# Half products in banks of their own, and q's low part behind the scans, in a hybrid decoder layer on Trainium2

## The chip, the cores and the metric

The kernel runs on one core of a Trainium2 chip. A core has a matmul engine (PE, with PEld for its weight loads), a vector engine (DVE), a scalar engine (ACT), a general engine (POOL) and a sync engine (SP), which here issues nearly all DMAs. Each engine works through its own instructions in order, and waits on semaphores for the others. SBUF is the memory on the chip; the results of matmuls go to PSUM, which is divided into banks. The metric is the device time of one execution in microseconds (us).

## The reference

One layer over 1024 tokens with 16 meta tokens ahead (1040 positions) and width 1024. After a norm, one projection feeds two groups of heads, 16 heads of an SSD (a state space scan in chunks of 128) and 16 heads of attention. An output projection over both and a convolutional FFN of width 2816 follow. The change lies in the projections q, k, v and in the attention, which has no softmax: each key takes its share of what the keys nearer to the query have left.

```python
xn = rms_norm(h, mix_pre_g[l])
proj = xn @ w_in[l]
q = proj[..., OFF_Q:OFF_K].reshape(Bsz, L, SB_HEADS, SB_HEAD_DIM)
...
    def block(args):
        i, qi = args
        ...
        zlog = jnp.einsum('bqhd,bkhd->bhqk', qi, kp) * scale
        log_beta = jax.nn.log_sigmoid(zlog)
        log_keep = jnp.where(valid, log_beta - zlog, 0.0)
        after = lax.cumsum(log_keep, axis=3, reverse=True) - log_keep
        w = jnp.where(valid, jnp.exp(log_beta + after), 0.0)
        return jnp.einsum('bhqk,bkhd->bqhd', w, vp)
...
mix = jnp.concatenate([y_ssd, y_sb], axis=-1) @ w_out[l]
h = h + rms_norm(mix, mix_post_g[l])
```

## The kernel before, in words

**Precision.** Matmuls take operands in a rounded 32-bit form. Where one product would be too coarse, an operand is split into a high part (a rounded copy, by ACT) and a low part (the rest, by DVE or POOL), and three products are added: high by high, high by low, low by high. So x, the weights, q and k all come as pairs (`wh`/`wl`, `qh`/`ql`, `kh`/`kl`).

**Stages.** Up to about 40 us x is loaded and normed. From 40 to 158 us come the convolved inputs of the SSD and its gate z for the first half of its heads; from 158 to 300 us the first scan of the SSD, with projections of the second half between; from 335 to 458 us its second scan, with the first 35 steps of the q, k, v products between. From 454 to 939 us the attention of the head pairs 0 to 6 runs, with the other q, k, v steps as filling; from 939 to 1018 us that of pair 7, with products of the output projection as filling. The rest of the output projection and the FFN follow to the end at 1855 us; the change does not touch them.

**The q, k, v products.** q, k and v of eight head pairs are 24 products of 1024 x 128 weights with x, taken two at a time as a `Blocks` object, twelve in all. Each goes by a scheme with 7 half-size products in place of 8. Products 1, 2 and 3 use x as it stands in SBUF (resident); 6, 5, 7 and 4 use sums of parts of x, `t2`, `t1`, `t3` and `t4`. These `x_sums` are worked out once, ahead of the first scan, written to DRAM (`xt13`, `xt42`), and streamed back through a ring of two places, each loaded in two halves (`load_half`, line 398); a matmul step asks for the next half when it has used one. Each product has two column halves of 260, so a block has 14 steps of 12 matmuls. The order of products is that of the list `QKV`: 1, 2, 6, 5, 3, 7, 4. Products 2, 5, 3 and 4 need sums of others: some are added in DVE when a PSUM bank is emptied, others by matmuls that go on in a bank that is kept. For k, the high part is copied from the bank by ACT and the low part taken by DVE (line 473) from the bank.

**Weights of a block.** `load` (line 407) brings 512 KB for each of the two, `split_a`, `sums`, `split_s12`, `split_s34` and `split_a22` make the weights of the products from them: the high part by ACT (line 413), the low part by POOL (line 414), sums by DVE (lines 429 to 432). A buffer of raw weights is loaded anew when POOL has taken the last low part from it.

**Attention.** For pair p and block i of 128 queries, `block_weights` multiplies q's block with all keys up to it (z, line 940; three products for each of two heads, in chunks of keys; 7 ends in two groups of chunks). ACT makes two sigmoids of each z (`kp` line 941, `bt` line 942). `split_q` takes the parts of the next block's q (`qh` on ACT, `ql` on DVE, line 917). DVE runs along the keys for the two heads (the scans, line 948), and POOL multiplies (line 950). Two blocks later `block_turn` transposes `bt` (`tw`, line 962), ACT copies it (`th`, line 964), and `block_mix` multiplies it with v (line 977). `edge_turn` and `edge_mix` do the meta keys, and store a pair's result (line 1001).

**Order.** PE's order in the attention is written out by hand, by the order of the code: `manual_schedule` for PE alone. On DVE, ACT, POOL and SP a scheduler orders the instructions.

Of the kernel before, what the change touches and what calls it, by code (L numbers as in the profile page):

```python
# [44 lines left out]
QKV = [(1, "a11", "b11", True), (2, "a12", "b21", False), (6, "s2", "t2", True), (5, "s1", "t1", True),  # L45
       (3, "s4", "b22", False), (7, "s3", "t3", True), (4, "a22", "t4", False)]
# [11 lines left out]
def tile_layer(ctx: ExitStack, tc: tile.TileContext, x, meta, rows, parts,  # L58
# [292 lines left out]
    def behind(*engines):  # L351
        st = ExitStack()
        traced = nc.cur_bb.bb.instructions
        for e in engines:
            last = next((i for i in reversed(traced) if i.engine == e), None)
            if last is not None:
                st.enter_context(tc.issue_after(last))
        return st

    def x_sums(k):  # L360
        rs = []

        def add_up():
            rs.extend(rp.tile([P, 2, HT], F32R, tag="rkl", name=f"xr{j}_{k}", bufs=3).bitcast(F32) for j in range(2))
            r1, r2 = rs
            with behind(ET.Pool):
                for r, kk in ((r1, k), (r2, k + 4)):
                    nc.gpsimd.tensor_tensor(r, xq[:, kk, :, 0].bitcast(F32), xq[:, kk, :, 1].bitcast(F32), op=ALU.add)
                nc.gpsimd.tensor_tensor(r1[:, 0], r1[:, 1], r1[:, 0], op=ALU.subtract)
                nc.gpsimd.tensor_tensor(r1[:, 1], r2[:, 1], r1[:, 1], op=ALU.subtract)  # L370

        def split():
            r1, r2 = rs
            with behind(ET.DVE, ET.Activation):
                nc.vector.tensor_tensor(r2[:, 1], r2[:, 1], r1[:, 0], op=ALU.subtract)
                nc.vector.tensor_tensor(r2[:, 0], r2[:, 0], r2[:, 1], op=ALU.subtract)
                for r, dst, nm in ((r1, xt13, "13"), (r2, xt42, "42")):
                    h = rp.tile([P, 2, HT], F32R, tag="rk", name=f"xh{nm}_{k}", bufs=3)
                    lo = r.bitcast(F32R)
                    nc.scalar.activation(h, r, AF.Copy)  # L380
                    nc.vector.tensor_tensor(lo, r, h.bitcast(F32), op=ALU.subtract)
                    for j, s in enumerate((h, lo)):
                        nc.sync.dma_start(out=dst[:, :, :, k, j, :],
                                          in_=s.bitcast(F32).rearrange("p t (c n) -> p t c n", n=HP))

        return add_up, split

    ring = [xq[:, 0:4, 1].rearrange("p k b n -> p k (b n)")[:, :, 2 * HP * s:2 * HP * s + 2 * HP] for s in range(2)]
# [3 lines left out]
    def load_half():  # L392
        u, h = divmod(loaded[0], 2)
        if u < len(units):
            loaded[0] += 1
            (src, j), c = t_of[units[u][0]], units[u][1]
            ks = slice(2 * h, 2 * h + 2)
            nc.sync.dma_start(out=ring[u % 2][:, ks].bitcast(F32), in_=src[:, j, c, ks].rearrange("p k b n -> p k (b n)"))

    class Blocks:  # L400
        def __init__(self, f1, f2, n):
            self.n, self.src, self.w = n, [{"q": w_q, "k": w_k, "v": w_v}[f][p] for f, p in (f1, f2)], {}
            self.f, self.r, self.late = (f1, f2), [None, None], []
# [21 lines left out]
        def sums(self):  # L425
            r1, r2 = self.r
            self.s2 = rp.tile([P, 4, P], F32, tag="s2", name=f"s2_{self.n}", bufs=1)
# [36 lines left out]
        def part(self, j, th, c):  # L464
            a = HT * th + HP * c
            if self.f[j][0] == "k":
                return [t[:, a:a + HP] for t in self.d[j]]
            return self.d[j][:, a:a + HP]

        def keep_k(self, th, c, a):  # L470
            kh, kl = self.part(0, th, c)
            acts = [lambda: nc.scalar.activation(kh, a, AF.Copy),
                    lambda: nc.vector.tensor_tensor(kl, a, kh.bitcast(F32), op=ALU.subtract)]
            if th == 0:
                acts.pop(0)()
            self.late += acts

        def step(self, s):
            (n, wn, xn, first), c = QKV[s // 2], s % 2
            if s == 0:  # L480
                self.d = [None, self.dest(1)]
            if s == 2:
                self.d[0] = self.dest(0)
            if first:
                self.acc = getattr(self, "acc", {})
                self.acc[c] = psum_mm(f"pj{n}_{self.n}_{c}")
            acc = self.acc[c]
            hi, lo = self.w[wn]
            if xn[0] == "t":
                rv = ring[used[0] % 2].rearrange("p k (b n) -> p k b n", b=2)  # L490
                used[0] += 1
            else:
                kk, th = {"b11": (0, 0), "b21": (4, 0), "b22": (4, 1)}[xn]
                rv = xq[:, kk:kk + 4, th, :, HP * c:HP * c + HP]
            for k in range(4):
                for j, (w, b) in enumerate(((hi, 0), (hi, 1), (lo, 0))):
                    mm(acc[:, :HP], w[:, k, :], rv[:, k, b, :], start=first and k == 0 and j == 0,  # L497
                       stop=k == 3 and j == 2, skip_group_check=not first)
                if xn[0] == "t" and k % 2:
                    load_half()  # L500
            for act in self.late:
                act()
            self.late = []
            add, a = nc.vector.tensor_tensor, acc[:, :HP]
            c11 = self.part(0, 0, c) if n in (2,) else None
# [1554 lines left out]
```

## Time and profile before

| what | value |
|---|---|
| median of 3 runs | 1852.49 us (1851.43 to 1856.2) |
| profiled execution, own time | 1856.6 us |
| its span, first to last instruction | 1854.8 us |
| mean granted clock of PE | 0.968 |
| PE busy | 1729.7 us (93%) |
| DVE, ACT, POOL busy | 1233.3, 856.6, 972.9 us |
| scans L948, 128 instructions | 209.4 us on DVE |
| products L950, 128 instructions | 210.2 us on POOL |
| q, k, v matmuls L497, weights `whis` | 768 instructions, 169.9 us |
| ring loads of x-sums | 192 loads of 520 KB |

A row of a timeline has the start in us from the span's beginning, the length in us, engine, line, operation, the tiles (written <- read), their shapes, and how many stand together; in brackets is how long the engine was idle before it, and what ended that. Rows of groups have busy time and mean duration in ns, and after the next bar the idle time ahead of them. Rows of waits have the sum, the number of times and the longest, in us. In rows of the profile, `kp`, `q` and `xall` are names without their numbers; the ring lies in `xall`, and the streamed sums are `xt`.

### The profile page before, as it was taken

What the parts mean: (1) busy time and instruction counts of PE and PEld (TensorE: products, weight loads), DVE (VectorE), ACT (ScalarE), POOL (GpSimd) and SP (SyncE); (2) the same over time, 40 slices, a digit from 0 to 9 for tenths busy, and PEclk for the clock granted to TensorE, in tenths of its full rate; (3) what the DMA queues carried; (4) which work ended last, traced back from release to release, by engine and by line L of the source; (5) the groups of instructions that cost most, each with busy time, mean ns of one, the idle gap of its engine ahead of it and who ended that gap; (6) DMA issues with size and microseconds to landing.
All of it is one profiled execution on the core that took longest, in us unless ns stands there. A gap on an engine that the chain in (4) does not pass through costs nothing. (4 is left out here: it accounts for less than half of the span.)

```text
span 1854.8 us, 29414 instructions
## 1 busy us (share of the span) xinstructions
PE 1729.7 (93%) x11518; PEld 1508.0 (81%) x11518; DVE 1233.3 (66%) x1360; ACT 856.6 (46%) x1474; POOL 972.9 (52%) x697
## 2 busy tenths in 40 slices
PE   7999899997888889888899999999999999999998
PEld 6998789876777788777767877898888999888786
DVE  5765884776658758768764056766666666657777
ACT  5424463543555656546665234543333333334544
POOL 4365664575657747667546212458677777600001
PEclk9999899998999989999999999999999999999999
DMA  4235443677665556655722354423223333187335
GB/s 153 69 109 177 146 132 103 206 251 244 216 199 185 196 158 200 218 201 192 239 92 83 133 198 148 137 69 117 95 86 92 118 103 104 61 270 251 103 97 187
DMA packets 151354, 284.73 MB, mean 154 GB/s; under 512 B 14032, under 2 KB 47336, under 8 KB 151216
## 3 DMA queue, kind: packets, MB, share of 16 engines
q1 hardware_dynamic: 151216, 282.85, 46.3%
q8 instruction: 91, 1.49, 0.3%
q14 instruction: 47, 0.39, 0.1%
HBM read 224.56 MB, written 58.25 MB: 152 GB/s over the span
## 5 line engine op out<-in xcount | busy, mean ns | idle before, releaser
L950 POOL TENSOR_TENSOR bt<-bt,kp 128x256 f32<-128x256 f32 (+7 forms) x128 | 210.2, 1660 | 139.9 <-DVE kp L948 110.3
L948 DVE TENSOR_TENSOR_SCAN kp<-kp,hold 128x272 f32<-128x272 f32 (+7 forms) x128 | 209.4, 1676 | 64.6 <-ACT kp L941 47.6
L497 PE MATMUL pj<-xall,whis 128*128 128x260 f32 x768 | 169.9, 319 | 53.0 <-DMA xall<-xt 35.1
L497 PEld LDWEIGHTS pj<-xall,whis 128*128 128x128 f32 x768 | 131.3, 209 | 69.3 <-issue 26.0
L1413 POOL TENSOR_TENSOR wlo<-wr,whi 128x1024 fp32r<-128x1024 f32 x43 | 109.2, 2551 | 37.2 <-ACT whi L1412 37.2
L497 PE MATMUL pj<-xall,whia 128*128 128x260 f32 x576 | 116.3, 300 | 10.2 <-DMA xall<-xt 6.2
L1917 POOL TENSOR_TENSOR fms<-fms 128x1 f32<-128x1 f32 x8 | 2.7, 334 | 223.7 <-DMA ar<-fda 187.5
L497 PE MATMUL pj<-xall,wlos 128*128 128x260 f32 x384 | 116.2, 303 | 0.0
L941 ACT ACTIVATE kp<-z 128x288 f32<-128x288 f32 (+6 forms) x112 | 82.5, 737 | 67.5 <-PE z L940 33.0
L497 PEld LDWEIGHTS pj<-xall,whia 128*128 128x128 f32 x576 | 89.8, 192 | 21.0 <-issue 6.0
L1412 ACT ACTIVATE whi<-wr 128x1024 fp32r<-128x1024 f32 x43 | 45.6, 1060 | 112.5 <-PE fX L1470 68.1
L160 PE MATMUL pj_X<-xall,wh_X 128*128 128x320 f32 (+1 forms) x384 | 96.9, 338 | 0.0
L1542 DVE SCALAR_TENSOR_TENSOR ga<-gr,pp,ga 128x1024 f32<-128x1024 f32 x44 | 71.4, 1622 | 34.0 <-ACT ga L1535 33.1
L964 ACT ACTIVATE th<-tw 128x1024 f32<-128x1024 f32 (+2 forms) x96 | 75.8, 815 | 39.2 <-PE tw L962 37.9
L160 PE MATMUL pj_z<-xall,wh_z 128*128 128x306 f32 (+2 forms) x384 | 92.4, 327 | 0.0
L1802 ACT ACTIVATE dh<-ar 128x512 fp32r<-128x512 f32 x77 | 48.5, 630 | 92.5 <-PE dnB L1880 44.7
L1803 DVE TENSOR_TENSOR dl<-ar,dh 128x512 fp32r<-128x512 f32 x77 | 53.2, 691 | 50.4 <-ACT dh L1802 50.3
L1119 PE MATMUL mo<-xall,yh 128*128 128x512 f32 x256 | 85.7, 402 | 0.0
L962 PE MATMUL tw<-ident,bt 128*128 128x128 f32 x576 | 78.7, 280 | 5.4 <-ACT bt L942 3.1
L942 ACT ACTIVATE bt<-z 128x288 f32<-128x288 f32 (+6 forms) x112 | 82.8, 740 | 0.0
L497 PE MATMUL pj<-xall,wloa 128*128 128x260 f32 x288 | 81.7, 284 | 0.0
L497 PEld LDWEIGHTS pj<-xall,wlos 128*128 128x128 f32 x384 | 80.3, 209 | 0.0
(579 smaller groups left out, 5752.6 us busy)
## 6 DMA issues: line engine op xcount, KB each, us to landing
xall<-xt SPq DMA_DIRECT2D x192, 520.0 KB
wr<-in_w_up SPq DMA_DIRECT2D x44, 512.0 KB
fds<-ga SPq DMA_DIRECT2D x44, 256.0 KB
b<-in_w_down SPq DMA_DIRECT2D x44, 256.0 KB
ar<-fds SPq DMA_DIRECT2D x44, 256.0 KB
fda<-ga SPq DMA_DIRECT2D x33, 256.0 KB
ar<-fda SPq DMA_DIRECT2D x33, 256.0 KB
yk<-yd SPq DMA_DIRECT2D x16, 512.0 KB
```

Source lines behind the costliest of these rows:

```text
L160: mm(acc[:ncol, :n - s], a[:, k, :ncol], x_cols(k, b, c0 + s, n - s), start=(k == 0 and j == 0), stop=(k == KB - 1 and j == 2))
L497: mm(acc[:, :HP], w[:, k, :], rv[:, k, b, :], start=first and k == 0 and j == 0, stop=k == 3 and j == 2, skip_group_check=not first)
L941: nc.scalar.activation(kp[:, :, a:a + w], z[:, :, :w], AF.Sigmoid, scale=-QSCALE)
L942: nc.scalar.activation(bt[:, :, a:a + w], z[:, :, :w], AF.Sigmoid, scale=QSCALE)
L948: nc.vector.tensor_tensor_scan(kp[:, j][:, ::-1], kp[:, j][:, ::-1], hold[:, L - n:L][:, ::-1], 0.0, op0=ALU.mult, op1=ALU.max)
L950: nc.gpsimd.tensor_tensor(bt[:, j, 0:m], bt[:, j, 0:m], kp[:, j, 1:m + 1], op=ALU.mult)
L962: nc.tensor.transpose(tw[:, j, b, :], bt[:, j, c0:c0 + P], ident)
L964: nc.scalar.activation(th[:, :, :nb, :], tw[:, :, :nb, :], AF.Copy)
L1119: mm(acc, u[:, k, :], v[:, cs], start=(k == 0 and j == 0), stop=(k == 7 and j == 2))
L1413: nc.gpsimd.tensor_tensor(l, raw, h.bitcast(F32), op=ALU.subtract)
L1542: nc.vector.scalar_tensor_tensor(v, self.g[jj][:, :, i:i + 256], fconv_w[:, j, i:i + 1], v, op0=ALU.mult, op1=ALU.add)
L1803: sub(lo[:, k], raw, hi[:, k].bitcast(F32), op=ALU.subtract)
```

## The change

- The products come in the order 6, 5, 3, 7, 1', 4, 2', two columns halves each, where 1' and 2' are the next block's. The first block's products 1 and 2 run ahead. Each product has a PSUM bank of its own; the sums between products are made by DVE adds when the bank is emptied.
- k's two halves are added into an SBUF tile `ks`; ACT copies its high part, 520 columns at once, and POOL takes the low part.
- `load`, the splits and the sums of the next block's weights stand at other steps. A half of the ring is one stretch of 4160 bytes per partition, where it was two of 2080.
- `x_sums` is wholly on DVE, and the code asks for it in the stage ahead of the scan.
- In the attention the written order counts for PE, DVE, ACT and POOL (`ORDERED`); SP's stays with the scheduler. `split_q` of the next block stands behind the scans. The store of a pair's result is put off to a later place in the loop.

```diff
     def x_sums(k):
-        rs = []
-        def add_up():
...
-        def split():
...
+        tag, dt_, w = (("rkl", F32R, L), ("rq", F32, L + 3))[k % 2]
+        r1, r2 = (rp.tile([P, w], dt_, tag=tag, name=f"xr{j}_{k}", bufs=3)[:, :L].bitcast(F32)
+                  .rearrange("p (t n) -> p t n", t=2) for j in range(2))
+        op2 = nc.vector.tensor_tensor
+        for r, kk in ((r1, k), (r2, k + 4)):
+            op2(r, xq[:, kk, :, 0].bitcast(F32), xq[:, kk, :, 1].bitcast(F32), op=ALU.add)
...
-    ring = [xq[:, 0:4, 1].rearrange("p k b n -> p k (b n)")[:, :, 2 * HP * s:2 * HP * s + 2 * HP] for s in range(2)]
+    ring = [xq[:, a, 1].rearrange("p b n -> p (b n)") for a in range(4)]
...
+        def keep_k(self, th, c, a, term):
+            if c == 0:
+                self.ks = rp.tile([P, HT], F32, tag="s2", name=f"ks{th}_{self.n}", bufs=1)
+            nc.vector.tensor_tensor(self.ks[:, HP * c:HP * c + HP], a, term, op=ALU.add)
+            if c == 1:
+                kh, kl = (t[:, HT * th:HT * th + HT] for t in self.d[0])
+                nc.scalar.activation(kh, self.ks, AF.Copy)
+                nc.gpsimd.tensor_tensor(kl, self.ks, kh.bitcast(F32), op=ALU.subtract)
...
-            if first:
-                self.acc = getattr(self, "acc", {})
-                self.acc[c] = psum_mm(f"pj{n}_{self.n}_{c}")
-            acc = self.acc[c]
+            acc = psum_mm(f"pj{n}_{self.n}_{c}")
...
+            for dst, term in {6: ((c21, c21),), 5: ((c22, c21),), 7: ((c22, c22), (c21, c21)), 4: ((c21, c21),)}[n]:
+                nc.vector.tensor_tensor(dst, a, term, op=ALU.add)
...
         for n, b in enumerate(blocks):
+            row = [(b, 6), (b, 5), (b, 3), (b, 7)] + ([(nxt, 1), (b, 4), (nxt, 2)] if nxt else [(b, 4)])
+            acts = {1: [b.split_a22]}
...
+                acts.update({4: [nxt.split_a], 7: [nxt.sums], 9: [nxt.split_s12], 12: [nxt.split_s34]})
+            if n and nxt:
+                acts[2] = [lambda: nxt.load(0)]
+                acts[5] = [lambda: nxt.load(1)]
...
-        nxt = (p, i + 1) if i < NT - 1 else (p + 1, 0)
-        if nxt[0] in heads:
-            split_q(*nxt)
         m = n - NM
         for j in range(2):
             nc.vector.tensor_tensor_scan(kp[:, j][:, ::-1], kp[:, j][:, ::-1], hold[:, L - n:L][:, ::-1], 0.0,
...
         turn.append((p, i, bt))
+        nxt = (p, i + 1) if i < NT - 1 else (p + 1, 0)
+        if nxt[0] in heads:
+            split_q(*nxt)
...
-        nc.sync.dma_start(out=yd1[:, :, p, :].rearrange("t d c -> d t c"), in_=ysc)
+        stores.append(lambda: nc.sync.dma_start(out=yd1[:, :, p, :].rearrange("t d c -> d t c"), in_=ysc))
...
-    pe_order.enter_context(tc.manual_schedule(engines={mybir.EngineType.PE}))
+    pe_order.enter_context(tc.manual_schedule(engines=ORDERED))
...
             run(block)
+            while stores:
+                stores.pop()()
```

DVE in the attention of pair 5. In the names, the first number is the pair (of `pj`, the product) and the second the block; `kp` rows are the two scans, `ql` is q's low part, `q7` and `vt6` are evacuations of q, k, v products. Before:

```order
L948 SCALAR_TENSOR_TENSOR kp5_4_8583<-kp5_4_8583,hold_4355 128x656 x2
L917 TENSOR_TENSOR ql5_6_8677<-q5_6831,qh5_6_8676 128x128
L948 SCALAR_TENSOR_TENSOR kp5_5_8656<-kp5_5_8656,hold_4355 128x784 x2
L514 TENSOR_TENSOR q7_8543<-pj6_10_0_8693,q7_8543 128x260
L917 TENSOR_TENSOR ql5_7_8761<-q5_6831,qh5_7_8760 128x128
L514 TENSOR_TENSOR q7_8543<-pj6_10_1_8720,q7_8543 128x260
L948 SCALAR_TENSOR_TENSOR kp5_6_8740<-kp5_6_8740,hold_4355 128x912 x2
```

and now:

```order
L937 SCALAR_TENSOR_TENSOR kp5_4_8659<-kp5_4_8659,hold_4374 128x656 x2
L909 TENSOR_TENSOR ql5_5_8685<-q5_6827,qh5_5_8684 128x128
L491 TENSOR_TENSOR vt6_8694<-pj2_10_0_8695,q7_8537 128x260
L491 TENSOR_TENSOR vt6_8694<-pj2_10_1_8722,q7_8537 128x260
L937 SCALAR_TENSOR_TENSOR kp5_5_8736<-kp5_5_8736,hold_4374 128x784 x2
L909 TENSOR_TENSOR ql5_6_8762<-q5_6827,qh5_6_8761 128x128
L494 TENSOR_TENSOR q7_8537<-pj6_10_0_8773,q7_8537 128x260
L494 TENSOR_TENSOR q7_8537<-pj6_10_1_8800,q7_8537 128x260
L937 SCALAR_TENSOR_TENSOR kp5_6_8820<-kp5_6_8820,hold_4374 128x912 x2
L909 TENSOR_TENSOR ql5_7_8846<-q5_6827,qh5_7_8845 128x128
```

Before, the low part of block 6 stood ahead of the scans of block 5; now it stands right behind them.

SP, which issues the loads, around the weights of block 10 (`wr0` and `wr1` are its two raw weights, rows with `xt13` and `xt42` the ring's halves, `yd1` a stored result). Before:

```order
L398 DMA xall_126<-xt13_109 128x2x520 x8
L1001 DMA yd1_92<-ysc3_6974 128x8x128
L398 DMA xall_126<-xt42_110 128x2x520 x8
L407 DMA wr0_10_8122<-in_w_v 128x1024
L558 DMA mvd_111<-v5_8017 16x128
L407 DMA wr1_10_8334<-in_w_q 128x1024
L398 DMA xall_126<-xt13_109 128x2x520 x8
```

and now:

```order
L993 DMA yd1_92<-ysc3_7030 128x8x128
L380 DMA xall_126<-xt42_110 128x1040 x8
L529 DMA mvd_111<-v5_8122 16x128
L389 DMA wr0_10_8342<-in_w_v 128x1024
L380 DMA xall_126<-xt13_109 128x1040 x4
L389 DMA wr1_10_8453<-in_w_q 128x1024
L380 DMA xall_126<-xt13_109 128x1040 x4
```

No load of the ring stood between the two weight loads; now four do.

DVE at the start of the first scan, whose first operations are `xdt`, `xw` and `cbm`; `xr` and `xh` belong to `x_sums`, with k as the second number. Before:

```order
L642 COPY xtk0_3_1215<-tt_X03_2_1225 128x512
L375 TENSOR_TENSOR xr1_0_1320<-xr1_0_1320,xr0_0_1319 128x520
L376 TENSOR_TENSOR xr1_0_1320<-xr1_0_1320 128x520
L794 TENSOR_TENSOR xdt0_0_1591<-xk0_0_1564,dt_652 16x512
L820 TENSOR_TENSOR xw0_0_1715<-xdt0_0_1591,dec_676 16x512
L794 TENSOR_TENSOR xdt0_1_1657<-xk0_1_1630,dt_652 128x512
L381 TENSOR_TENSOR xr0_0_1319<-xr0_0_1319,xh13_0_1413 128x1040
```

and now:

```order
L365 CAST xh13_3_1554<-xr0_3_1546 128x1040
L361 TENSOR_TENSOR xr1_3_1547<-xr1_3_1547 128x520
L366 TENSOR_TENSOR xr0_3_1546<-xr0_3_1546,xh13_3_1554 128x1040
L365 CAST xh42_3_1559<-xr1_3_1547 128x1040
L366 TENSOR_TENSOR xr1_3_1547<-xr1_3_1547,xh42_3_1559 128x1040
L788 TENSOR_TENSOR xdt0_0_1591<-xk0_0_1564,dt_652 16x512
L814 TENSOR_TENSOR xw0_0_1715<-xdt0_0_1591,dec_676 16x512
```

Before, the sums of k = 0 were begun when the scan began; now those of the last k = 3 end ahead of it.

More of the change, by code (lines that the diff above doesn't have):

```diff
@@ L499, in step @@
                 if xn[0] == "t" and k % 2:
                     load_half()
[L501 to L505, printed above, removed]
+            a = acc[:, :HP]
             c21, c22 = self.part(1, 0, c), self.part(1, 1, c)
@@ L572, in qkv_flow, with turn_next @@
         post = []
+        def turn_next():
+            act = post.pop(0) if post else None
+            if act:
+                act()
+        first = blocks[0]
+        for n in (1, 2):
+            for c in range(2):
+                first.step(n, c)
+                if n == 2 and c == 0:
+                    first.split_s34()
+                yield
         for n, b in enumerate(blocks):
@@ L1221, in tile_layer @@
     edge_mix(7, edge)
+    stores.pop()()
     run(meta_steps)
```

167 lines of the change are left out of this document (68 added, 99 removed).

## The prediction, made before the changed kernel ran

> **What bounds the kernel now.** I read the table of windows first, to find the stages in which PE (the matmul engine) has room. Its columns are the window, its length, the busy time of PE, of its weight loads, of DVE, ACT and POOL, the granted clock, and the DMA engines' share and rate.
>
> ```profile
> 100.00:165.00 65.00, 62.02 (x392) 60.92 (x390) 34.19 (x24) 15.98 (x25) 36.55 (x19) 0.97 0.43 142
> 165.00:230.00 65.00, 53.15 (x298) 46.13 (x299) 53.61 (x47) 34.57 (x67) 44.25 (x29) 0.84 0.48 149
> 458.00:936.00 478.00, 411.45 (x3641) 368.86 (x3641) 345.29 (x381) 276.79 (x504) 312.20 (x222) 0.93 0.60 199
> 936.00:1020.00 84.00, 81.68 (x603) 60.92 (x601) 42.95 (x38) 48.59 (x87) 45.37 (x35) 0.98 0.24 77
> ```
>
> From 458 to 936 us (attention of the pairs 0 to 6, with the q, k, v products as fill) PE is idle for 478.00 - 411.45 = 66.6 us. At a mean clock of 0.93 it also loses 0.07 x 411.45 = 28.8 us. So 95 us is the most that this stage could give up while PE's work stays the same. From 165 to 230 us (start of the first scan of the SSD half) the same count gives 11.9 + 8.5 = 20.4 us. Against that, 100 to 165 us shows an undisturbed stretch: 3.0 + 1.9 = 4.9 us. The last window has only 2.3 us idle.
>
> Second, the waits of PE from 458 to 936 us, by what came last (sum, times, longest), and the waits of SP's sequencer, which issues the loads, from 335 to 936 us:
>
> ```profile
> PE pj L497 <- DMA xall<-xt: 39.0, 24, 5.7
> PE pj L497 <- DVE kl L473: 14.4, 9, 2.9
> ...
> SPq L407 <- POOL wlos L414: 61.9, 10, 12.5
> SPq L407 <- POOL wloa L414: 57.6, 7, 16.1
> ```
>
> PE waits mostly for the ring of x-sums (39.0 us), then for k's low part, which frees a PSUM bank (14.4 us). Behind the ring stands SP: it is parked for 61.9 + 57.6 us at weight loads whose buffer POOL's split has yet to leave, and the ring's loads queue behind them. The timeline has such a case, SP first, then PE (start, length, engine and line):
>
> ```profile
> 590.19 0.35 SPq L407 DMA_DIRECT2D wr<-in_w_q  x1
> 590.63 1.92 SPq L398 DMA_DIRECT2D xall<-xt  x4
> 595.35 0.77 PE L497 MATMUL pj<-xall,whis 128*128 128x260 f32 x2 [5.47 <-DMA xall<-xt]
> ```
>
> The weight load goes at 590.19, four ring loads follow at once, and PE starts at 595.35 after 5.47 us of idleness.
>
> **The change part by part.** *Ring, banks, weight loads: -95 us at most.* The streamed products now alternate with resident ones, so a ring half has two more steps to arrive. Each product owns its bank, and DVE adds the parts afterwards, so k's low part holds no bank any more. Between the two weight loads of a block, and before the first, more ring loads go first, as the order of SP shows. I take the whole 95 us out and put back what remains: 9 us of ring and bank waits (at least 4; at most 25, about half of 39.0 + 14.4).
>
> *The cost of own banks.* DVE has 168 evacuations for 152, 16 more. The row of the same size:
>
> ```profile
> L473 DVE TENSOR_TENSOR kl<-pj,kh 128x260 fp32r<-128x260 f32 x26 | 10.9, 418 | 3.1 <-ACT kh L472 3.1
> L368 POOL TENSOR_TENSOR xr<-xall 128x1040 f32<-128x1040 f32 x8 | 21.7, 2722 | 6.5 <-DMA xt<-xr 5.2 <-DVE em L791 1.3
> ```
>
> 16 x 0.418 = 7 us lie beside PE, DVE being busy for 345 of 478 us; I cost them at nothing, 7 us if the cover is gone. k's high part on ACT now comes behind two such adds, and what is queued on ACT behind it waits too, the sigmoids of a z block among them. 16 halves x 0.42 = 6.7 us; I take 6 (2 to 10). POOL gets 16 subtractions of 520 columns, at half of the second row's 2.72 us some 22 us in all. POOL is busy for 312 of 478 us and nobody needs k's low part before the next pair: nothing, and within the 2 to 10 if that fails.
>
> *q's low part behind the scans: +79 us.* Before, q's low part for block i+1 stood on DVE between the scans of i-1 and of i. Now it stands behind the two scans of block i, and since DVE works in written order, PE's z of block i+1 waits for it. That closes a loop: z of i, sigmoids on ACT, two scans, low part of q, z of i+1. I read its length from the timeline of before. PE's z rows (start of z for i = 4, the low-part matmul in it, then i = 5, 6; after the break i = 6, 7 and 0 of the next pair):
>
> ```profile
> 836.91 0.42 PE L940 MATMUL z<-kh,qh 64*128 64x328 f32 x2
> 837.17 0.32 PE L940 MATMUL z<-kh,ql 64*128 64x328 f32 x2
> 842.33 0.45 PE L940 MATMUL z<-kh,qh 64*128 64x392 f32 x2
> 848.35 0.48 PE L940 MATMUL z<-kh,qh 64*128 64x456 f32 x2
> ...
> 779.74 0.47 PE L940 MATMUL z<-kh,qh 64*128 64x456 f32 x2
> 787.23 0.42 PE L940 MATMUL z<-kh,qh 64*128 64x348 f32 x2
> 794.92 0.34 PE L940 MATMUL z<-kh,qh 64*128 64x144 f32 x2
> ```
>
> and DVE's scans (both of a block in one row) and low parts:
>
> ```profile
> 839.77 4.81 DVE L948 TENSOR_TENSOR_SCAN kp<-kp,hold 128x656 f32<-128x656 f32 x2 [1.50 <-ACT kp L941]
> 844.50 1.34 DVE L917 TENSOR_TENSOR ql<-q,qh 128x128 fp32r<-128x128 f32 x1
> 845.76 4.59 DVE L948 TENSOR_TENSOR_SCAN kp<-kp,hold 128x784 f32<-128x784 f32 x2
> 850.59 0.97 DVE L917 TENSOR_TENSOR ql<-q,qh 128x128 fp32r<-128x128 f32 x1
> ...
> 783.49 4.70 DVE L948 TENSOR_TENSOR_SCAN kp<-kp,hold 128x912 f32<-128x912 f32 x2 [0.39 <-ACT kp L941]
> 793.04 5.22 DVE L948 TENSOR_TENSOR_SCAN kp<-kp,hold 128x1040 f32<-128x1040 f32 x2 [0.45 <-ACT kp L941]
> 798.50 0.98 DVE L917 TENSOR_TENSOR ql<-q,qh 128x128 fp32r<-128x128 f32 x1
> ```
>
> The first z matmul needs no low part, so 837.17 - 836.91 = 0.26 us comes off each loop. Start of z to start of scans, plus scans, plus low part, minus 0.26, against the distance of z starts, at which PE was filled throughout:
> i = 4: 2.86 + 4.81 + 1.34 - 0.26 = 8.75 against 5.42, 3.33 too long.
> i = 5: 3.43 + 4.59 + 0.97 - 0.26 = 8.73 against 6.02, 2.71 too long.
> i = 6: 3.75 + 4.70 + 0.97 - 0.26 = 9.16 against 7.49, 1.67 too long.
> i = 7: 5.81 + 5.22 + 0.98 - 0.26 = 11.75 against 7.69, 4.06 too long.
> Together 11.8 us per pair. The blocks 0 to 3 I leave out: their scans are shorter and PE has as much to do. The scans vary, so I also read the groups' means of one scan, and the shortest pairs of scans:
>
> ```profile
> L948 DVE TENSOR_TENSOR_SCAN kp<-kp,hold 128x1040 f32<-128x1040 f32 x12 | 33.9, 2863 | 3.4 <-ACT kp L941 3.4
> L948 DVE TENSOR_TENSOR_SCAN kp<-kp,hold 128x912 f32<-128x912 f32 x14 | 33.4, 2426 | 0.6 <-ACT kp L941 0.4 <-issue 0.2
> L948 DVE TENSOR_TENSOR_SCAN kp<-kp,hold 128x656 f32<-128x656 f32 x14 | 29.7, 2157 | 7.9 <-ACT kp L941 6.0 <-issue 1.9
> L948 DVE TENSOR_TENSOR_SCAN kp<-kp,hold 128x784 f32<-128x784 f32 x14 | 26.9, 1958 | 4.0 <-ACT kp L941 2.1 <-POOL bt L950 1.8
> ...
> 558.82 2.92 DVE L948 TENSOR_TENSOR_SCAN kp<-kp,hold 128x656 f32<-128x656 f32 x2
> 712.36 3.47 DVE L948 TENSOR_TENSOR_SCAN kp<-kp,hold 128x784 f32<-128x784 f32 x2
> 719.91 4.00 DVE L948 TENSOR_TENSOR_SCAN kp<-kp,hold 128x912 f32<-128x912 f32 x2
> 868.89 4.53 DVE L948 TENSOR_TENSOR_SCAN kp<-kp,hold 128x1040 f32<-128x1040 f32 x2
> ```
>
> Twice the means sum to 18.8 us, where the example's scans sum to 19.3: 11.3 us per pair, for seven pairs 79 us. The shortest sum to 14.9: 7.4 per pair, 52 us. The upper end has a low part of 1.34 us in every block: 90 us. I take the means, since POOL's products run beside these scans as before.
>
> *The clock: +20 us.* The new waits bring some of the clock loss back. The window that follows a wait of PE, and that wait:
>
> ```profile
> 544.50 0.48 PE L497 MATMUL pj<-xall,whis 128*128 128x260 f32 x2 [2.38 <-DMA xall<-xt]
> ...
> 546.00:549.50 3.50, 3.37 (x20) 3.04 (x20) 1.18 (x3) 1.28 (x2) 0.87 (x2) 0.51 1.03 374
> ```
>
> After 2.38 us of idleness the clock drops to 0.51 from 546.0 to 549.5, which costs 0.49 x 3.37 = 1.65 us. The blocks 4, 5 and 7 have new waits longer than this one, 21 in seven pairs: 35 us if each brings such a stretch, 12 us if only those of block 7 do. I take 12 stretches, 20 us.
>
> [...]
>
> *The x-sums before the first scan: -11 us.* They leave POOL (eight additions of 2.72 us, the second row above, and eight of half the size) and ACT, and stand on DVE in the stage before, where DVE is busy for 34.2 of 65 us. The scan's start then has POOL, ACT and DVE to itself. By L473's 0.418 us for 260 columns, the six operations of 1040 columns and four of 520 of one k take at most 6 x 1.67 + 4 x 0.84 = 13.4 us, 53 us for the four, the fixed part of each counted four times over. DVE has 31 us free from 100 to 165, and some of these operations ran there before. So most fits, and the rest runs into the scan's start as it did. The ends are the 20.4 - 4.9 = 15.5 us by which the scan's window is worse than the undisturbed one, and 0 if what was lost there was the scan's own chain. I take -11, nearer to the first, since three engines are cleared and only one is loaded.
>
> *The rest.* 35 of the 168 q, k, v steps run beside the second scan: zero, between -6 and +6. In pair 7, ACT's split of the output weights now stands in written order ahead of sigmoids and may wait for its DMA: between 0 and two of the longest waits above, 11 us; I take 3. The deferred store of the attention rows only moves on SP.
>
> *Sum:* -95 + 9 + 6 + 79 + 20 = +19 in attention, -11 at the first scan, +3 at the end: +11 us. The profiled execution took 1856.6 us, so it would be 1867.6. It lies 4 us above the median of the runs, 1852.5, to which I add the same 11: 1864 us.
>
> **The rivals.** *Faster: the loop is short.* DVE runs scans at their shortest and ACT delivers as early as in the rows above. Then the loop costs 52 us, the clock 12: -95 + 9 + 6 + 52 + 12 - 11 + 3 = -24, which is 1828 us. For it: such scans are in the rows. Against: no reason why all should be like that. It decides where the loop takes less than 68 us, 9.7 per pair.
>
> [...]
>
> *The written order ties ACT to DMA and DVE, or the weight loads go on parking SP.* Here the change fails to do what it says. Half of the old waits stay (25 for 9), k's and the output weights' terms go to their upper ends (10 and 11), scan 0 gains 3: +11 + 16 + 4 + 8 + 8 = +47 us, 1900 us. For it: in-order ACT has many producers; against it: the weight loads stand further behind the split that frees their buffer.
>
> **How the numbers follow.** 0.3% (5.6 us) is about what a measurement of this kernel can tell from no change. The likeliest case, a loop that eats the whole gain, has 0.44; the short loop 0.30; the holding clock 0.08; the tied order 0.14; another balance within 0.3% 0.04. So faster 0.30, same 0.12, slower 0.58. The likeliest case's own range is 1858 to 1885. The range that takes in the rivals goes from the short loop's 1828 to a little above the tied order's 1900: 1828 to 1905.
>
> **What would show it.** Right: PE's waits for the ring fall from 39 to under 15 us, those for k's low part vanish, and waits of z for q's low part appear, 2 to 4 us each in the blocks 4 to 7, some 79 us. The distance of z starts for i = 7 grows from 7.7 to about 11.7 us. SP's time at the weight loads falls well below 120 us. Between 165 and 230 us PE is busy for 58 us or more. Wrong: if z starts follow at the old distances, the loop isn't closed, and then the time falls by more than 24 us; if the ring's waits stay, SP was not the cause.

## The result: 1.3% slower

The changed kernel takes 1879.23 us in the median of 3 runs (1874.86 to 1880.74), against 1852.49 us before: a ratio of 1.0134, 95% interval 1.01 to 1.0169. Its profiled execution is that of 1874.86 us, with a span of 1873.1 us and a mean granted clock of 0.969. It is 18.3 us longer than the profiled execution of before; the medians differ by 26.7 us.

The windows of the kernel after, first the start of the first scan, then attention from the z of pair 0 to that of pair 7 (the columns are those of the table in the prediction):

```profile
165.00:230.00 65.00, 64.67 (x422) 56.87 (x421) 55.60 (x55) 36.66 (x70) 43.87 (x31) 1.00 0.35 98
421.20:953.40 532.20, 440.86 (x3684) 389.10 (x3684) 327.96 (x395) 276.92 (x493) 307.07 (x244) 0.90 0.53 181
```

and attention of before between the same two points:

```profile
453.50:938.90 485.40, 418.31 (x3684) 375.01 (x3684) 349.67 (x388) 282.09 (x512) 315.65 (x232) 0.93 0.60 199
```

The scan's window, with 53.15 us of PE before, is now full, at full clock. Attention begins 32.3 us earlier and ends 14.5 us later: with the same 3684 matmuls it takes 532.2 us in place of 485.4. PE's idle time there rises from 67.1 to 91.3 us, and the clock loss from 0.07 x 418.31 = 29 to 0.10 x 440.86 = 44 us. The clocks in these rows are rounded to two places; by busy time, the same matmuls take 22.5 us more, and with the 24.2 us of idle time that is the whole 46.8.

By stages (start of the first matmul of each, from the two traces): at the end of the second half's B and C the changed kernel is 22.6 us ahead (334.61 against 312.05 us, the last matmul of C); beside the second scan it wins 9.7 more; attention loses 46.8; from pair 7 to the FFN's first matmul it loses 4.6; the FFN is equal within 0.8. The sum is +18.3 us.

PE's waits in the kernel after, from 415 to 960 us (sum, times, longest), and those of SP from 335 to 960 us:

```profile
PE z L932 <- DVE ql L909: 57.5, 27, 6.0
PE z L932 <- ACT th L956: 17.9, 11, 3.4
PE z L932 <- DVE zk L843: 5.6, 1, 5.6
...
PE pj L478 <- DMA xall<-xt: 3.8, 8, 0.8
```

```profile
SPq L389 <- POOL wlos L396: 41.3, 8, 10.3
...
SPq L389 <- POOL wloa L396: 13.4, 5, 5.0
```

The ring's 39.0 us are down to 3.8, the 14.4 us of k's low part are gone, SP stands 54.7 us at the weight loads in place of 119.5. In their place stands a wait that the kernel before does not have: z for q's low part, 57.5 us in 27 waits. The longest ones come once per pair, at the first block behind block 7: these seven sum to 33.6 us, and the waits in z of the blocks 5, 6 and 7 to 3.0, 12.0 and 7.1. One of the long ones, DVE first, then POOL, then PE from the z of block 7 on:

```profile
794.22 4.64 DVE L937 TENSOR_TENSOR_SCAN kp<-kp,hold 128x1040 f32<-128x1040 f32 x2 [1.56 <-ACT kp L933]
798.78 2.02 DVE L909 TENSOR_TENSOR ql<-q,qh 128x128 fp32r<-128x128 f32 x1
...
796.81 5.84 POOL L939 TENSOR_TENSOR bt<-bt,kp 128x1024 f32<-128x1024 f32 x2 [2.35 <-DVE kp L937]
...
786.28 0.43 PE L932 MATMUL z<-kh,qh 64*128 64x348 f32 x2
...
795.99 0.34 PE L932 MATMUL z<-kh,qh 64*128 64x144 f32 x2
800.85 0.49 PE L932 MATMUL z<-kh,ql 64*128 64x144 f32 x2 [4.53 <-DVE ql L909]
```

PE begins z at 795.99 with the high part, then stands for 4.53 us until DVE has ended two scans and the low part. The low part begins while the first of POOL's two products runs, and ends at 800.80, 0.15 us after that product (800.65 in the trace, where the two have rows of their own).

### The profile page after: what moved, and what is told of

It reads as the page before. It is cut to its first block, busy times and chain, and to the rows that moved or that the text cites. A ratio compares the mean times of both kernels' runs of the same rounds, so it can differ in the third digit from the quotient of the medians.

```text
span 1873.1 us, 29436 instructions
## 1 busy us (share of the span) xinstructions
PE 1736.8 (93%) x11518; PEld 1511.3 (81%) x11518; DVE 1216.5 (65%) x1400; ACT 842.5 (45%) x1442; POOL 932.0 (50%) x697
## 3 DMA queue, kind: packets, MB, share of 16 engines
q8 instruction: 91, 1.49, 0.3%
## 5 line engine op out<-in xcount | busy, mean ns | idle before, releaser
L937 DVE TENSOR_TENSOR_SCAN kp<-kp,hold 128x272 f32<-128x272 f32 (+7 forms) x128 | 184.6, 1483 | 106.1 <-ACT kp L933 79.8
L478 PE MATMUL pj<-xall,whis 128*128 128x260 f32 x768 | 162.6, 310 | 8.3 <-DMA xall<-xt 6.7
L478 PEld LDWEIGHTS pj<-xall,whis 128*128 128x128 f32 x768 | 126.9, 203 | 23.1 <-issue 8.7
L969 PE MATMUL av<-th,v 128*64 128x128 f32 x1152 | 95.3, 322 | 0.0
L932 PE MATMUL z<-kh,ql 64*128 64x144 f32 (+6 forms) x224 | 41.8, 369 | 57.7 <-DVE ql L909 57.5
L160 PE MATMUL pj_X<-xall,wh_X 128*128 128x320 f32 (+1 forms) x384 | 92.8, 327 | 0.0
L969 PEld LDWEIGHTS av<-th,v 128*64 128x64 f32 x1152 | 77.2, 162 | 15.5 <-issue 13.1
```

Of the source, the lines that this page charges most:

```text
L160: mm(acc[:ncol, :n - s], a[:, k, :ncol], x_cols(k, b, c0 + s, n - s), start=(k == 0 and j == 0), stop=(k == KB - 1 and j == 2))
L478: mm(acc[:, :HP], w[:, k, :], rv[k][:, b, :], start=k == 0 and j == 0, stop=k == 3 and j == 2)
L937: nc.vector.tensor_tensor_scan(kp[:, j][:, ::-1], kp[:, j][:, ::-1], hold[:, L - n:L][:, ::-1], 0.0, op0=ALU.mult, op1=ALU.max)
L969: mm(av[halves[j], :], v[:, kb, halves[j]], th[:, j, b, :], start=kb == 0, stop=kb == i)
```

## The experiments

Times are compared as ratios to the kernel before, run on the same chip in the same series (its medians there are 1855 to 1856 us).

**The loop undone.** The q parts are written ahead of the scans again; all else is as changed.

```diff
+        nxt = (p, i + 1) if i < NT - 1 else (p + 1, 0)
+        if nxt[0] in heads:
+            split_q(*nxt)
         m = n - NM
         for j in range(2):
             nc.vector.tensor_tensor_scan(...)
...
         turn.append((p, i, bt))
-        nxt = (p, i + 1) if i < NT - 1 else (p + 1, 0)
-        if nxt[0] in heads:
-            split_q(*nxt)
```

> The changed kernel with one thing undone: the next block's q parts are written ahead of the block's scans again, still in written order on all four engines. Theory (the loop through q's low part is what costs): PE's waits of z for q's low part, 57.5 us in 27 waits, fall below 8 us, the clock loss in the attention falls by half of its 44 us, and the time falls by 55 to 80 us against the changed kernel, to 1800 to 1825 us. Rival (a wait of another kind takes the place, for instance z for the copies of th on ACT, 17 us now): these waits grow by 20 us or more, and the time falls by less than 30 us, to 1850 us or more.

1837.3 us, ratio 0.991 (0.9892 to 0.9927): 42 us faster than the changed kernel and faster than before. Waits for q's low part are gone. So moving the q parts behind the scans is what makes the change slower. But the fall lies between the two expectations. The window of attention and PE's waits (415 to 960 us) show why:

```profile
422.10:912.40 490.30, 417.28 (x3684) 372.05 (x3684) 305.85 (x396) 276.25 (x493) 313.01 (x244) 0.94 0.57 197
```

```profile
PE z L932 <- ACT th L956: 26.5, 11, 6.3
PE pj L478 <- DVE q L494: 12.2, 5, 4.8
PE pj L478 <- DMA xall<-xt: 8.5, 13, 2.2
PE vtc L524 <- DVE edge L519: 5.7, 1, 5.7
PE vtp L512 <- DVE vt L494: 5.2, 2, 3.4
```

Attention takes 490.3 us, not less than the 485.4 of before, although the ring's waits are down from 39 to 8.5. PE is idle for 73.0 us and loses 0.06 x 417 = 25 us to the clock: 98 us, as much as the 96 of before. z's waits for th, evacuations and the ring share what the ring and the banks alone had.

**Written order for PE alone.**

```diff
-    pe_order.enter_context(tc.manual_schedule(engines=ORDERED))
+    pe_order.enter_context(tc.manual_schedule(engines={mybir.EngineType.PE}))
```

> The changed kernel with the written order for PE alone in the attention; DVE, ACT and POOL are ordered by the scheduler again, which puts q's low part ahead of the scans by itself. Theory (loop): as with the q parts ahead, waits for q's low part below 8 us, 1800 to 1830 us. Rival (the written order on ACT and DVE is what frees banks and ring in time): waits for k's and v's evacuations and for the ring come back with 20 us or more, 1845 us or more.

1826.07 us, ratio 0.9837 (0.9822 to 0.9852), as the loop theory expected. The scheduler puts q's low part ahead of the scans although the code has it behind, and no wait of z for it is left. The rival's waits did come back in part: 19.6 us for the ring, 25.5 us for the evacuations by DVE of `q`, `ks` and `vt`. They were just not dearer than what the written order costs.

**The x-sums alone, in the kernel before.** The old `x_sums` and its `posts` are replaced by the changed ones.

```diff
-        parts_ = [x_sums(k) for k in range(4)]
-        posts = [[parts_[0][0]], [parts_[0][1], parts_[1][0]], [parts_[1][1], parts_[2][0]],
-                 [parts_[2][1], parts_[3][0], parts_[3][1]]]
+        posts = [[lambda k=k: x_sums(k)] for k in range(4)]
```

> The kernel before with the changed x-sums alone (all on DVE, asked for one stage earlier). Theory: the 22 us that the changed kernel is ahead when the second half's B and C are done come from the x-sums alone, so this kernel is 17 to 24 us faster than before, 1829 to 1836 us, with PE busy for over 60 of the 65 us from 165 to 230 us. Rival (the gain came from other things in that stage, or the ring's own late start takes it back): less than 8 us faster, 1845 us or more.

1833.37 us, ratio 0.9876 (0.9856 to 0.9895): 22 us faster, as expected. Its windows show the whole gain ahead of attention, and attention as before:

```profile
165.00:230.00 65.00, 64.63 (x422) 56.81 (x422) 55.60 (x55) 36.64 (x70) 43.94 (x31) 1.00 0.35 98
431.20:919.10 487.90, 421.75 (x3684) 377.95 (x3684) 350.11 (x388) 282.13 (x512) 314.69 (x232) 0.92 0.59 198
```

Against this kernel, all the rest of the change with q's parts ahead (1837.3 us) gains nothing.

**Products 4 and 1' exchanged,** on top of the q parts ahead of the scans.

```diff
-            row = [(b, 6), (b, 5), (b, 3), (b, 7)] + ([(nxt, 1), (b, 4), (nxt, 2)] if nxt else [(b, 4)])
+            row = [(b, 6), (b, 5), (b, 3), (b, 7)] + ([(b, 4), (nxt, 1), (nxt, 2)] if nxt else [(b, 4)])
```

> The changed kernel with the q parts ahead of the scans, and besides with products 4 and 1' exchanged, so that products 7 and 4 follow each other as before (four streamed steps, then four resident ones). Theory (the ring was late because SP was parked at weight loads, which now go when their buffer is free): PE's waits for the ring stay below 12 us in the attention, and the time is within 6 us of the kernel with the q parts ahead. Rival (turn and turn about of streamed and resident products is what gives the ring time): ring waits of 20 us or more, 15 us or more slower.

1848.29 us, ratio 0.9964: 11 us slower than with turns, between the two theories. The waits for the ring are 16.6 us in place of 8.5, and SP stands 111 us at weight loads where it stood 73. So the turns help both the ring and the loads; the two causes aren't separated by this run. Nor does most of the time lie there: of the 11.3 us between the two profiled executions 7.4 come beside the second scan (from C's last matmul to the first z 116.9 us in place of 109.5), where the ring's waits are under 1 us in both, and 4.2 in attention.

**Written order in the kernel before.**

```diff
-    pe_order.enter_context(tc.manual_schedule(engines={mybir.EngineType.PE}))
+    pe_order.enter_context(tc.manual_schedule(engines=ORDERED))
```

> The kernel before with one thing changed: the written order holds for PE, DVE, ACT and POOL in the attention (its code has the q parts ahead of the scans). Theory (the written order makes ACT and DVE wait for one another, and gives back what the ring and the banks save): z's waits for the copies of th rise from 2 us to 15 us or more, and it is 5 to 20 us slower than before, 1858 to 1875 us. Rival (the written order costs nothing by itself): within 4 us of before.

1880.88 us, ratio 1.0125 (1.0101 to 1.015): 24 us slower with the old products and the q parts ahead. The size is above the expected range, and the place is another: z's waits for th are only 9.2 us.

```profile
PE vtc L553 <- DVE edge L551: 24.3, 5, 7.3
PE pj L497 <- DVE kl L473: 22.8, 10, 4.2
PE pj L497 <- DMA xall<-xt: 14.3, 20, 1.8
```

The transposition of v's edge waits 24.3 us for a copy that the written order puts behind scans and evacuations on DVE. The change has that copy earlier (`keep_edge`), so it needs this part where the order is written. The ring's waits fall here too, without any of the ring's edits, from 39.0 to 14.3 us, and SP's time at the weight loads from 119.5 to 91.5. PE is late for other reasons, and the ring may catch up meanwhile; that this is why isn't shown.

**Which engine's written order costs.** With the q parts ahead, the written order holds for PE and DVE, or for PE and ACT.

```diff
-    pe_order.enter_context(tc.manual_schedule(engines=ORDERED))
+    pe_order.enter_context(tc.manual_schedule(engines={mybir.EngineType.PE, mybir.EngineType.DVE}))
```

> The changed kernel with the q parts ahead of the scans, and the written order for PE and DVE alone; ACT and POOL are ordered by the scheduler. Theory (ACT's written order is what costs there, by k's high part and the like standing ahead of th and the sigmoids): z's waits for th fall from 26 us to below 10, the time from 1837 to 1815 to 1828 us. Rival (DVE's order is what costs): th waits below 10 too, but evacuation waits of 30 us or more, and 1832 us or more.

> As the last, but the written order for PE and ACT alone, DVE and POOL by the scheduler. Theory (ACT's order costs): z's waits for th stay at 18 us or more, 1832 us or more. Rival (DVE's order costs): 1828 us or less.

PE and DVE: 1826.91 us, ratio 0.9847 (0.9822 to 0.9872), with 12.5 us of z's waits for th, more than the 10 that the theory allowed. So the written order of ACT or of POOL costs the 10 us, since both are the scheduler's here; the last run below finds no cost in POOL's. The ring's waits are 22.0 us, where all four orders gave 8.5, though SP stands at the weight loads about as long (80.9 and 73.3 us). So part of the ring's fall comes with the written order, and not with the order of the products. PE and ACT: 1861.4 us, ratio 1.0019 (1.0001 to 1.0038), which fits the theory's time, but not for its reason: th is at 10.6 us, and the scheduler, given ACT's order, lets PE wait for q's low part again.

```profile
PE z L932 <- DVE ql L909: 35.7, 25, 4.6
```

35.7 us of this wait stand beside 34.5 us of time against PE and DVE. The two kernels differ in the order of two engines, so this agrees with the price of the loop without showing it again.

**What stands in ACT's way.** With the q parts ahead, ACT waits 36.4 us at k's high part. One case of it:

```profile
470.44 0.30 ACT L972 ACTIVATE ysc<-av 128x128 f32<-128x128 f32 x1
477.34 0.64 ACT L457 ACTIVATE kh<-ks 128x520 fp32r<-128x520 f32 x1 [6.59 <-DVE ks L454]
477.88 1.28 ACT L956 ACTIVATE th<-tw 128x1024 f32<-128x1024 f32 x2
...
478.94 0.66 PE L932 MATMUL z<-kh,qh 64*128 64x348 f32 x2 [6.33 <-ACT th L956]
```

k's high part waits for DVE's add, which stands behind scans; th waits behind it on ACT; z needs the bank that th empties. Here the split of k is written two steps later.

```diff
-                nc.scalar.activation(kh, self.ks, AF.Copy)
-                nc.gpsimd.tensor_tensor(kl, self.ks, kh.bitcast(F32), op=ALU.subtract)
+                ks = self.ks
+                def split_k():
+                    nc.scalar.activation(kh, ks, AF.Copy)
+                    nc.gpsimd.tensor_tensor(kl, ks, kh.bitcast(F32), op=ALU.subtract)
+                late.append([2, split_k])
```

> The changed kernel with the q parts ahead of the scans, all four engines in written order, and the split of k (high part on ACT, low part on POOL) written two steps later, where its sum is long done. Theory (ACT stands 36 us at k's high part behind DVE's adds, and th and the sigmoids behind it): ACT's waits there fall below 12 us, z's waits for th by 8 us or more, and the time falls by 8 to 18 us, to 1819 to 1829 us. Rival (these waits have cover, or others take their place): 1833 us or more.

1833.15 us, ratio 0.9877: 4 us faster, within what the two intervals leave open. The waits for th fell from 26.5 to 10.0 us as the theory said; evacuations of `q` and `vt` took the place (14.5 + 6.6 us for 12.2 + 3.1). The rival is nearer.

**q's parts ahead of z.** What was late next was DVE: it stood 84.5 us at q's low part for q's high part, which ACT makes behind four sigmoids. Beside the late split of k, the parts are asked for ahead of z (the last block of a pair stays as it was).

```diff
+        if i < NT - 1:
+            split_q(p, i + 1)
         n = NM + (i + 1) * P
...
-        nxt = (p, i + 1) if i < NT - 1 else (p + 1, 0)
-        if nxt[0] in heads:
-            split_q(*nxt)
+        if i == NT - 1 and p + 1 in heads:
+            split_q(p + 1, 0)
```

> As the kernel with k's split written two steps later, and besides q's parts of the next block are written ahead of the block's z, so that q's high part on ACT comes ahead of the sigmoids (for the last block of a pair it stays ahead of the scans). Theory (DVE stands 84 us at q's low part, because q's high part comes behind four sigmoids on ACT, and the scans and evacuations behind it are late): DVE's waits there fall below 25 us, PE's waits for evacuations of q and v by 8 us or more, and the time from 1833 to 1815 to 1826 us. Rival (that lateness is covered): within 5 us of 1833 us.

1815.68 us, ratio 0.9792 (0.9764 to 0.982): the fastest of all, 39 us below the kernel before and 64 below the changed one. DVE's wait (420 to 920 us) falls as expected, and attention, in the window behind it, is clearly shorter than before:

```profile
DVE ql L924 <- ACT qh L923: 18.9, 12, 2.3
```

```profile
420.00:890.00 470.00, 412.39 (x3683) 368.49 (x3684) 330.88 (x394) 276.19 (x492) 319.06 (x244) 0.94 0.59 205
```

PE's waits for evacuations, which were to fall by 8 us for q and v, fell by 3.5 (14.5 + 6.6 to 11.5 + 6.1), and by 5.8 with those of `ks` (4.3 to 2.0).

The same with written order for PE and DVE alone, and the q parts ahead of z, but with k's split at its changed place:

> The changed kernel with q's parts of the next block ahead of its z, written order for PE and DVE alone, k's split at its changed place. Theory: 1815 to 1825 us, a little below the 1827 us of the kernel without the early q parts, since the scheduler of ACT had put the high part early already in part. Rival (no change): 1825 to 1832 us.

1831.21 us, ratio 0.9879 (0.9846 to 0.9911): no gain over 1826.91, as the rival said. PE's waits are the same too (22.1 us for the ring after 22.0, 12.1 for th after 12.5). That the scheduler orders ACT without regard to the place in the code would fit this, but isn't shown.

**The loop with k's split late.** The last two kernels: the changed kernel with the late split of k as its only difference, and the fastest one with POOL left to the scheduler.

> The changed kernel with k's split written two steps later as the only difference (q's parts stay behind the scans). Theory (the loop through q's low part sets the attention's length, and other waits lie beside it): the 4 us that this edit gave where q's parts were ahead are not gained here, PE's waits for q's low part stay at 50 us or more, and the time is within 8 us of the changed kernel, 1871 to 1887 us. Rival (waits add up): the time falls by 10 us or more, since z's waits for th (17 us) go.

> The kernel with q's parts ahead of z and k's split late, with POOL left to the scheduler (PE, DVE and ACT in written order). Theory (POOL's order is no limit there): within 6 us of 1816 us. Rival (POOL's written order costs, since weight splits and k's low part stand ahead of the products after the scans): 1808 us or less.

The first takes 1874.13 us, ratio 1.0113 (1.0082 to 1.0144). z's waits for th fall from 17.9 to 11.8 us, and those for q's low part rise from 57.5 to 63.1: what the one gives up the other takes. The q parts behind the scans cost 41 us against the same kernel with them ahead (1833.15), as they did with the early split (42). The second takes 1821.71 us, ratio 0.982 (0.9802 to 0.9838): POOL's order is no limit, within 6 us.

## Why the prediction was right, and where its terms were not

The forecast was slower, 1864 us by the median, through a loop over q's low part; it is slower, 1879 us. The loop is there, and undoing it alone turns the sign. That the sum of +11 came near the +18.3 of the profiled executions is luck: attention came out 27.8 us dearer than forecast (46.8 for 19) and the stages ahead of it 21.3 us cheaper (32.3 us won for 11).

- **The loop, +79.** Measured 57.5 us of waits. The mechanism is right, the terms are not. By the means of the prediction seven pairs have 19.8, 14.3, 12.8 and 32.0 us for the blocks 4 to 7; the waits that follow them are 3.0, 12.0, 7.1 and 33.6 us. Block 4 failed most, because its row came from one pair. There z of block 5 started 5.42 us after z of block 4; over the seven pairs of before it is 7.2 us in the mean, and now 9.8, so that the loop has hardly anything to exceed. For block 7 each part was off and the errors cancel: in the case above start of z to scans takes 7.94 us for 5.81, the scans 4.64 for 5.22, the low part 2.02 for 0.98, between z starts 9.71 for 7.69.
- **The scans in the loop.** "I take the means, since POOL's products run beside these scans as before" is the reason that failed. DVE's groups after:

```profile
L937 DVE TENSOR_TENSOR_SCAN kp<-kp,hold 128x1040 f32<-128x1040 f32 x14 | 33.6, 2443 | 8.5 <-ACT kp L933 8.5
L937 DVE TENSOR_TENSOR_SCAN kp<-kp,hold 128x912 f32<-128x912 f32 x14 | 29.2, 2125 | 17.1 <-ACT kp L933 17.1
L937 DVE TENSOR_TENSOR_SCAN kp<-kp,hold 128x784 f32<-128x784 f32 x14 | 24.9, 1821 | 8.9 <-ACT kp L933 6.5 <-issue 2.4
L937 DVE TENSOR_TENSOR_SCAN kp<-kp,hold 128x656 f32<-128x656 f32 x14 | 22.9, 1676 | 20.6 <-ACT kp L933 16.4 <-POOL wlos L396 4.3
```

  Twice these means is 16.1 us per pair in place of 18.8. That would make the loop 60 us, but its nearness to 57.5 is luck again, since block 4 would still have 13 us. The long scans are those that began while POOL was in an operation. In the example of the prediction for i = 4, whose two scans took 4.81 us, POOL was in this addition:

```profile
839.38 2.40 POOL L1008 TENSOR_TENSOR sq<-sq,sqb 128x1024 f32<-128x1024 f32 x1
```

  The first scan began at 839.77 and took 3.39 us, the second 1.49. Of the 56 scans of these four widths (415 to 960 us) 23 are over 0.06 us longer than the shortest of their width before, and 12 now; in all 35 POOL was in an operation when the scan began (of the other 77, eleven began so, with 0.16 us or less of it left). So fewer scans meet one now. Scans during which an operation of POOL began, with none at their own begin, were not longer: 44 of the 112, all within 0.01 us of the shortest of their width; and with q's parts ahead, all fourteen scans of 1040 columns take 2.29 to 2.32 us (2.31 in the mean), half of them beside products. This is read from the traces; no run tries it by itself. In time, the loop costs 42 us, since the same waits hide others.
- **What remains of the old waits, 9 + 6 against 95 taken out.** This is the step that failed most. The ring's waits did fall to 3.8 us and those for k's low part went, but with q's parts ahead, and so without the loop, idleness and clock cost 98 us, not 15. The prediction asked what the ring and the banks leave, not what DVE's adds and ACT's written order, behind scans, put in their place: it costed DVE's 16 more adds at nothing "beside PE", while PE's waits for evacuations by DVE (`q`, `vt`, `ks`) and for th take the room there. The rival of the tied order had this mechanism, with 0.14. Of its conditions, ACT behind k's high part is shown (32.4 us of ACT's waits); the weight loads did not go on parking SP (54.7 us for 119.5).
- **The clock, +20.** Measured 44 us by the window. The term's low end, 12 us where only block 7's waits bring half clock, is further off: half clock followed a wait of 2.33 us in block 6 and one of 1.72 us for `vt`, below.
- **The x-sums, -11.** Measured -22.6 us up to the end of the second half's B and C, and -22 as a change by itself, outside the ends of 15.5 and 0. I held back part of the 15.5 us for the scan's own chain, but the x-sums brought all of it, and more even than the 20.4 us of that window. Their operations were shorter than L473's 0.418 us for 260 columns made them: on DVE those of 520 columns took 0.69 us for 0.84 (twelve of sixteen; the other four 1.22 in the mean), those of 1040 took 0.87 to 1.23 us for 1.67.
- **Beside the second scan, zero between -6 and +6.** Measured -9.7 us, outside the bounds. The x-sums alone don't bring it (119.1 us there for 118.9); the exchange of 4 and 1' gives 7.4 us back, so the order of the products has most of it.
- **Pair 7 and the output projection, +3.** Measured +4.6, and -0.8 in the FFN. ACT waits 10.1 us for the output weights' DMA, as the step said.
- **The rivals.** The short loop was half right, with short scans; it missed because the rest was not gained. For the holding clock, with its 0.08, no run shows a length of wait up to which the clock stays full: half clock followed single waits of 2.33 and 1.72 us, below.
- **The signs.** The ring's waits (3.8 us, under 15), SP's time at the weight loads and PE's 64.67 us from 165 to 230 us came as forecast. The distance of z starts for i = 7 did not grow from 7.7 to 11.7 us: it is 8.1 to 12.2, 9.7 in the mean against 8.4 before. z starts with its high part, as the sum itself had it, and the wait stands inside z.

## What to carry to other kernels

Before an operation is moved in an in-order queue, follow who needs its result next: here a short subtraction on DVE, set behind two scans, closed a loop that PE could not fill, and the change's own gain ahead of attention (32 us) was hidden by it. When waits are taken out of a full stage, don't count them as gained: look which wait ends only little before, since in this one 39 us of ring waits became waits of other kinds at the same total. And a written order for several engines has to be read on each of them: an operation that waits (k's high part) belongs behind those that others wait for, and one that all wait for (q's parts) goes ahead of the block's own work; with both, the same change is 2.1% faster than the kernel before.

## What the hardware showed unexpectedly

**The clock.** In the clock records of before and after all 94 changes lie on a grid of 3.413 us, and the falls went mostly with how busy PE was in the slice ahead of them. In the kernel after, three slices and the one behind each:

```profile
773.36:776.77 3.41, 1.08 (x10) 0.77 (x10) 2.87 (x3) 0.18 (x2) 3.41 (x2) 1.00 0.89 310
776.77:780.18 3.41, 3.41 (x25) 2.52 (x22) 0.76 (x1) 3.41 (x5) 3.17 (x4) 0.50 0.02 7
783.60:787.01 3.41, 1.70 (x16) 1.29 (x16) 2.60 (x4) 0.73 (x3) 3.41 (x2) 1.00 0.37 152
787.01:790.42 3.41, 3.41 (x29) 2.71 (x26) 0.00 (x0) 3.41 (x6) 2.71 (x3) 0.50 0.01 2
609.51:612.93 3.41, 2.16 (x19) 1.75 (x17) 1.79 (x3) 1.96 (x4) 3.00 (x4) 1.00 0.30 88
612.93:616.34 3.41, 2.46 (x24) 2.09 (x25) 0.59 (x1) 3.41 (x8) 3.41 (x3) 1.00 0.97 284
```

With 1.08 us (32%) and 1.70 us (50%) of PE busy, and one wait of 2.33 and of 1.72 us, the next slice ran at half clock; with 2.16 us (63%) it didn't. I laid the traces of all 14 kernels over the slices at which their clock records change (from 100 us on; busy is the union of the matmuls' spans). Of the slices at full clock with PE busy below 40%, all 165 were followed by half clock; between 40 and 60%, 84 of 202; at 60% and more, 23 of 6375 (in before and after alone 29 of 29, 17 of 28 and 1 of 906; a case or two moves between the groups with the way the grid is laid). In most slices of the first group PE had one wait; in eleven it had two or three, the longest of them 0.93 to 2.14 us, and these fell too (in after one at 933.8 us, with 1.16 and 1.24 us). Of the slices at half clock, those with full clock behind them were all busy for 80% or more (258 cases), and 23 as busy as that had half clock behind them again (in before and after alone 46 and 5, and none of 16 below 80% had full clock behind it). The share does not account for every fall: 21 of the 23 at 60% and more came behind slices busy for about 80% or more (the one in before, at 1085.3 us, for 88%), and why stays open. In attention the records show half clock for 69 us before, 103 us now and 63 us with q's parts ahead.

**DVE behind POOL.** In these traces a scan, or q's low part, that began on DVE while an operation ran on POOL was longer by about what was left of that operation. For the 35 long scans counted above, the excess over the shortest of the width is 0.11 us less (0.106 to 0.116) than what was left of POOL's operation at the scan's begin. In the kernel after, 62 of the 64 low parts began while POOL was at work, and each ended 0.14 to 0.15 us after that operation; they take 0.4 to 2.0 us, more from block to block (one 2.4), and the other two 0.26 and 0.28. With q's parts ahead of the scans 22 began so, and the mean of a low part is 0.65 us for 1.24. In the kernel before it was 63 of 64, so the 0.97 to 1.34 us that the forecast read there as the low part's work were mostly time beside an operation on POOL (the one low part that began beside none took 0.29), and the term grew to 2.02 us behind block 7, whose product is the longest.
